# Making all low pieces of weights on VectorE in the second mixer and in the first mixer's output product

## The chip, the cores and the metric

The kernel runs on one core of a Trainium2 chip. The metric is the device time of one execution in microseconds. In three runs the kernel before took 2084.22, 2087.37 and 2090.94 us; the median is 2087.37 us. The core has TensorE (matrix products), VectorE, ScalarE, GpSimd and SyncE, which here issues most of the transfers. The profile calls them PE, DVE, ACT, POOL and SP; PEld is TensorE's loading of weights.

## The reference, cut to what matters

A two-layer network works on 256 tokens of 2048 channels, with 256 more as context. Each layer has a mixer and a gated ConvFFN; both are preceded by an RMS norm with shift and scale, and multiplied by a gate, all of which come from a conditioning vector. Layer 0 has the first mixer, a convolution beside a state-space model; layer 1 has the second, a gated MLP over chunks of tokens:

```
def chunk_mlp_mixer(hn, w_in, ln_g, ln_b, sgu_w, sgu_b, w_out):
    z = jax.nn.gelu(hn @ w_in)
    u, v = jnp.split(z, 2, axis=-1)
    v = layer_norm(v, ln_g, ln_b)
    ...
    s = jnp.einsum('hqk,bnkhc->bnqhc', sgu_w.astype(v.dtype), v)
    ...
    return (u * s.reshape(bn, length, SGU_W)) @ w_out

sh1, sc1, g1, sh2, sc2, g2 = jnp.split(silu_c @ ada_w[layer] + ada_b[layer], 6, axis=-1)
h_lat = h_lat + g1[:, None, :] * mix
```

All is in 32-bit floats. `hn @ w_in` of the second mixer is 256 x 2048 by 2048 x 4096, its output product 256 x 2048 by 2048 x 2048. `silu_c @ ada_w` is one vector by 2048 x 12288 in each layer.

## The kernel before, in words

Every large product is done as three products of the faster 32-bit kind: a weight `raw` is split into a high piece `hi` (a rounded copy, ScalarE, line 129) and a low piece `lo` = `raw` - `hi` (line 132). The activations were split in the same way into `xh` and `xl` (or `ah` and `al`). TensorE then adds `xh` x `hi`, `xh` x `lo` and `xl` x `hi` (lines 136 to 138). A weight tile of 128 x 2048 is fetched by one transfer (line 156, four buffers `raw`) and is split in two halves of 128 x 1024, here called splits; `hi` and `lo` have three buffers each. Each split feeds twelve products: two tiles of 128 tokens, two column halves, three products.

A counter decides which engine makes a `lo`: every `pool_every`-th split goes to GpSimd, the others to VectorE. The value is set stage by stage in `even` and `program`: for the first three quarters of the first mixer's output product it is `PE3`, 4; from the first ConvFFN to the end of the program it is `PE5`, 2, so that the engines take turns.

Beside the splits VectorE does the norms, the state-space scans of the first mixer (line 766), the residual adds (lines 407, 408), the layer norm of `v` in the second mixer, and for three of the twelve conditioning vectors a product done by hand: slabs `rawa` of 128 x 1024 from `ada_w` (two buffers, line 239) are multiplied by the conditioning vector and added to `adacc` (line 241). The other conditioning vectors are done on TensorE (line 199).

A scheduler sets the order of instructions on each engine when the program is built, from priorities and modelled times: fetch and split of weights are raised by `ahead`, 200 or 250 places. Each engine, and the queue of SyncE that issues transfers, then works in that fixed order: an instruction that waits holds up all behind it.

Of the kernel before, what the change touches and what calls it, by code (L numbers as in the profile page):

```python
# [31 lines left out]
NB = LD // 2  # L32
PE1 = 3
PE2 = 1000000000
PE3 = 4
PE0 = 4
PE4 = 1000000000
ADA_G = 0
PE5 = 2
# [19 lines left out]
class Builder:  # L59
# [844 lines left out]
    def even(self):  # L904
# [157 lines left out]
        row = self.gate_row(0, 2)  # L1062
        self.pool_every = PE3
        self.out_proj(WO, h, row, mh, ml, q4[:3], None, (ADA_EO, 0.0), rate=RS[8])
# [232 lines left out]
    def program(self, stop=99):  # L1297
        nc, A = self.nc, self.A
        h, ssq = self.even()
        if stop == 1:  # L1300
            return dict(xh=self.mh, xl=self.ml)
        q4 = [(q, 4 * q) for q in range(4)]
        self.yp = self.ctx.enter_context(self.tc.tile_pool(name="yp", bufs=1))
        if stop == 2:
            return dict(h=h)
        self.pool_every = PE5
        self.ahead = AHEAD2
        for l in range(2):
            if l == 1:
                self.xh, self.xl = self.xpair()  # L1310
                self.ada_pump(ADA_B[1])
                self.norm_mod(h, ssq, 1, 0, self.xh, self.xl)
                ah = self.yp.tile([128, KT, 256], F32R, name="ah", tag="ah")
                al = self.yp.tile([128, KT, 256], F32R, name="al", tag="al")
                self.odd(ah, al)
                ssq = self.new_ssq()
                row = self.gate_row(1, 2)
                self.out_proj(A["o_w_out"], h, row, ah, al, q4, ssq, ADA_O2)
                if stop == 4:
                    return dict(h=h)  # L1320
            self.xh, self.xl = self.xpair()
            self.ada_pump(ADA_B[2 * l])
            self.norm_mod(h, ssq, l, 1, self.xh, self.xl)
            ssq = self.new_ssq()
            self.ffn(l, h, ssq, *(ADA_F0 if l == 0 else ADA_F1))
            if stop == 3 + 2 * l:
                return dict(h=h)
        with self.tc.high_priority(HP2):
            r = self.ssq_rms(ssq, D, "rn")
            for t in range(2):  # L1330
                for g in (0, 2):
                    c = slice(512 * g, 512 * g + 1024)
                    x = h[:, t, 512 * g:512 * g + 512]
                    nc.vector.tensor_scalar(x, x, r[:, t:t + 1], None, op0=OP.mult)
                    x = h[:, t, 512 * g + 512:512 * g + 1024]
                    nc.scalar.activation(x, x, AF.Copy, scale=r[:, t:t + 1])
                    nc.sync.dma_start(self.out[t, :, c], h[:, t, c])
# [98 lines left out]
```

## Time and profile before

| | us |
|---|---|
| median of three runs | 2087.37 |
| the profiled execution | 2086.91 |
| its span | 2085.1 |
| TensorE busy, whole span | 1979.5 |
| second mixer, 1156 to 1512 us: TensorE busy | 322.71 of 356 |
| second mixer: VectorE busy | 238.91 of 356 |
| second mixer: GpSimd busy | 127.65 of 356 |
| first mixer's product and scans, 380 to 515 us: TensorE busy | 125.39 of 135 |

All durations come from the one profiled execution. The second mixer's stage is bounded here by the norm ahead of it and the norm of the ConvFFN behind it. Where an idle time is given in brackets, the profile names what ended it. Transfers are named after the tile that they fill.

### The profile page before, as it was taken

Reading aid. Unit: us, or ns where it says so; the run is one execution under the profiler, and the core shown is the slowest. Engines: PE = TensorE matmul, PEld = TensorE weight load, DVE = VectorE, ACT = ScalarE, POOL = GpSimd, SP = SyncE. Lnnn points to the kernel's source line nnn. Section 1 sums busy time; section 2 is a strip of 40 time slices with the busy share of each in tenths; the row PEclk is TensorE's granted clock in tenths of the full one; section 3 lists DMA queues with packets and bytes.
Section 4 is the critical chain, followed back from the end, with each engine's and each line's share of the span. In section 5 each row is a group of like instructions: output and inputs, shape, how many; then the busy total and the mean of one; then the engine's idle time right before and its main releaser. Section 6 shows DMA issues by size and latency. Waiting matters only on the chain.

```text
span 2085.1 us, 26177 instructions
## 1 busy us (share of the span) xinstructions
PE 1979.5 (95%) x9736; PEld 1479.9 (71%) x9736; DVE 1407.6 (68%) x2444; ACT 961.4 (46%) x1320; POOL 724.8 (35%) x376
## 2 busy tenths in 40 slices
PE   5999999899899999999999899989899999999997
PEld 2567676567577677777777677767577888888886
DVE  6467376666768996367865757566747885378874
ACT  3354353734445453355544543333355554455553
POOL 4311143011043443444344334434233344444443
PEclk8999999999999999999999999999999999999999
DMA  9993553876886888656577788787866655555552
GB/s 383 400 356 123 196 194 142 320 287 245 302 323 254 293 328 322 246 219 222 207 257 264 270 308 301 272 302 263 322 241 230 232 181 193 183 187 188 190 201 102
DMA packets 85530, 523.66 MB, mean 251 GB/s; under 512 B 10679, under 2 KB 11112, under 8 KB 29720
## 3 DMA queue, kind: packets, MB, share of 16 engines
q1 hardware_dynamic: 82198, 517.84, 67.1%
q10 hardware_dynamic: 2820, 2.99, 0.4%
q8 instruction: 76, 1.25, 0.2%
q0 software_dynamic: 384, 1.16, 0.1%
q14 instruction: 52, 0.42, 0.1%
HBM read 519.83 MB, written 2.13 MB: 250 GB/s over the span
## 4 chain that ended last, share of the span: by engine, by line
PE 76%; DVE 10%; DMA 5%; issue 5%; ACT 2%; POOL 2%; ACTq 0%; SPq 0%; POOLq 0%; DVEq 0%
PE mm L136 21%; PE mm L137 21%; PE mm L138 21%; PE ad L199 4%; DVE lo L132 2%; DVE adacc L241 2%; POOL lo L132 2%; DMA rawa<-in_ada_w 2%; PE tp L1209 1%; PE ad L472 1%; PE tp L877 1%; DVE w L766 1%; PE ms L794 1%; DMA glub<-in_glu_b 1%; PE tp L738 1%
## 5 line engine op out<-in xcount | busy, mean ns | idle before, releaser
L132 POOL TENSOR_TENSOR lo<-raw,hi 128x1024 fp32r<-128x1024 f32 x253 | 628.7, 2485 | 1224.5 <-ACT hi L129 1202.7
L129 ACT ACTIVATE hi<-raw 128x1024 fp32r<-128x1024 f32 x568 | 598.8, 1059 | 823.8 <-PE mm L138 638.9
L137 PE MATMUL mm<-lo,xh 128*128 128x512 f32 x1632 | 644.9, 395 | 21.5 <-DVE lo L132 21.5
L136 PE MATMUL mm<-hi,xh 128*128 128x512 f32 x1632 | 656.6, 404 | 1.6 <-ACT hi L129 1.6
L138 PE MATMUL mm<-hi,xl 128*128 128x512 f32 x1632 | 643.4, 394 | 1.6 <-DVE xl L399 1.6
L132 DVE TENSOR_TENSOR lo<-raw,hi 128x1024 fp32r<-128x1024 f32 x315 | 402.4, 1281 | 323.8 <-ACT hi L129 323.2
L136 PEld LDWEIGHTS mm<-hi,xh 128*128 128x128 f32 x1632 | 307.9, 190 | 126.3 <-issue 56.5
L137 PEld LDWEIGHTS mm<-lo,xh 128*128 128x128 f32 x1632 | 309.8, 190 | 89.0 <-DVE lo L132 29.4
L138 PEld LDWEIGHTS mm<-hi,xl 128*128 128x128 f32 x1632 | 309.4, 190 | 69.8 <-DVE xl L399 2.4
L136 PE MATMUL mm<-hi,ah 128*128 128x512 f32 x640 | 256.0, 401 | 2.9 <-ACT hi L129 2.8
L137 PE MATMUL mm<-lo,ah 128*128 128x512 f32 x640 | 255.8, 400 | 2.5 <-DVE lo L132 2.4
L138 PE MATMUL mm<-hi,al 128*128 128x512 f32 x640 | 254.7, 398 | 0.0
L241 DVE SCALAR_TENSOR_TENSOR adacc<-rawa,cst,adacc 128x1024 f32<-128x1024 f32 x96 | 163.0, 1708 | 54.9 <-DMA rawa<-in_ada_w 52.2
L1225 DVE SCALAR_TENSOR_TENSOR ca<-tp,fcw,ca 128x189 f32<-128x189 f32 (+2 forms) x512 | 179.0, 419 | 28.4 <-ACT ca L1212 28.4
L1225 DVE SCALAR_TENSOR_TENSOR cg<-tp,fcw,cg 128x189 f32<-128x189 f32 (+2 forms) x512 | 179.3, 419 | 21.8 <-ACT cg L1212 21.8
L136 PEld LDWEIGHTS mm<-hi,ah 128*128 128x128 f32 x640 | 120.5, 189 | 47.4 <-issue 14.2
L137 PEld LDWEIGHTS mm<-lo,ah 128*128 128x128 f32 x640 | 121.0, 189 | 33.7 <-DVE lo L132 5.1
L138 PEld LDWEIGHTS mm<-hi,al 128*128 128x128 f32 x640 | 121.1, 189 | 30.3 <-issue 1.7
L199 PE MATMUL ad<-raw,cst 128*32 128x512 f32 x896 | 125.0, 605 | 0.9 <-DMA raw<-in_ada_w 0.9
L407 DVE TENSOR_TENSOR wk<-mm,grow 128x512 f32<-128x512 f32 x56 | 38.2, 684 | 47.0 <-PE mm L138 47.0
L1277 DVE TENSOR_TENSOR al<-ca,ah 128x512 fp32r<-128x512 f32 x32 | 53.4, 1669 | 19.8 <-ACT ah L1276 19.7
L408 DVE TENSOR_TENSOR h<-h,wk 128x512 f32<-128x512 f32 x56 | 55.2, 989 | 1.3
(272 smaller groups left out, 1430.4 us busy)
## 6 DMA issues: line engine op xcount, KB each, us to landing
raw<-in_ada_w SPq DMA_DIRECT2D x132, 1024.0 KB, 5.8
raw<-in_f_w_in SPq DMA_DIRECT2D x128, 1024.0 KB, 4.9
raw<-in_f_w_out SPq DMA_DIRECT2D x64, 1024.0 KB, 5.0
rawa<-in_ada_w SPq DMA_DIRECT2D x96, 512.0 KB, 5.7
raw<-in_o_w_in SPq DMA_DIRECT2D x32, 1024.0 KB, 6.0
raw<-in_e_w_in SPq DMA_DIRECT2D x28, 1024.0 KB, 7.1
raw<-in_e_w_out SPq DMA_DIRECT2D x16, 1024.0 KB, 5.1
raw<-in_o_w_out SPq DMA_DIRECT2D x16, 1024.0 KB, 7.4
```

Of the source, the lines that this page charges most:

```text
L129: nc.scalar.activation(hi, raw, AF.Copy)
L132: eng.tensor_sub(lo, raw, hi.bitcast(F32))
L136: nc.tensor.matmul(ps, xh, wh, start=first, stop=False)
L137: nc.tensor.matmul(ps, xh, wl, start=False, stop=False)
L138: nc.tensor.matmul(ps, xl, wh, start=False, stop=last)
L199: nc.tensor.matmul(st["ps"][32 * j:32 * j + 32, :], self.cst[:, kt], raw[:, 512 * j:512 * j + 512], start=kt == 0, stop=kt == KT - 1, tile ...
L241: nc.vector.scalar_tensor_tensor(a, raw, self.cst[:, kt, 0:1], a, op0=OP.mult, op1=OP.add)
L407: nc.vector.tensor_mul(m, ps[t], row[:, c])
L408: nc.vector.tensor_add(h[:, t, c], h[:, t, c], m)
L472: nc.tensor.matmul(st["ps"][32 * j:32 * j + 32, :n], self.cst[:, no * s + o], raw[:, c:c + n], start=s == 0 and o < 2, stop=s == 16 // no ...
L1225: nc.vector.scalar_tensor_tensor(oo, s[:, y0 + dy:y1 + dy, x0 + dx:x1 + dx], w, oo, op0=OP.mult, op1=OP.add)
L1277: nc.vector.tensor_sub(al[:, kt:kt + 2], a, ah[:, kt:kt + 2].bitcast(F32))
```

## The change

```
-PE3 = 4
+PE3 = 1000000000
...
+                self.pool_every = 10 ** 9
                 self.odd(ah, al)
                 ssq = self.new_ssq()
                 row = self.gate_row(1, 2)
                 self.out_proj(A["o_w_out"], h, row, ah, al, q4, ssq, ADA_O2)
                 if stop == 4:
                     return dict(h=h)
+            self.pool_every = PE5
             self.xh, self.xl = self.xpair()
```

With a `pool_every` that the counter never reaches, all `lo` of the first mixer's output product and of the second mixer (input product, `odd`, and output product) are made on VectorE. The counter itself goes on, so that the ConvFFNs divide their splits as before. No instruction is added or removed; but the scheduler sets a new order.

On VectorE, in the first mixer's output product, where the residual of one group of columns (`wk`, `h`) meets the scans (line 766) of the state-space part:

```order
 L766 SCALAR_TENSOR_TENSOR w<-s5q,w 128x128
 L408 TENSOR_TENSOR h<-h,wk 128x512
-L766 SCALAR_TENSOR_TENSOR w<-s5q,w 128x128 x2
-L132 TENSOR_TENSOR lo<-raw,hi 128x1024
-L766 SCALAR_TENSOR_TENSOR w<-s5q,w 128x128 x2
+L132 TENSOR_TENSOR lo<-raw,hi 128x1024 x2
+L766 SCALAR_TENSOR_TENSOR w<-s5q,w 128x128 x6
```

Two low pieces stand where one stood, ahead of two scans that stood ahead of it.

On VectorE, in the second mixer, in the chain of small steps that makes the layer norm's factor `rnr`:

```order
 L319 SCALAR_TENSOR_TENSOR rnr<-rnt,rnj 128x2
 L317 TENSOR_TENSOR rnt<-rnr 128x2
+L132 TENSOR_TENSOR lo<-raw,hi 128x1024
 L318 SCALAR_TENSOR_TENSOR rnt<-rnt,ov 128x2
 L319 SCALAR_TENSOR_TENSOR rnr<-rnt,rnr 128x2
```

A low piece now stands in the middle of the chain.

On VectorE, towards the end of the second mixer's output product, before the change:

```order
L241 SCALAR_TENSOR_TENSOR adacc<-rawa,cst,adacc 128x1024 x2
L132 TENSOR_TENSOR lo<-raw,hi 128x1024
L241 SCALAR_TENSOR_TENSOR adacc<-rawa,cst,adacc 128x1024 x2
L132 TENSOR_TENSOR lo<-raw,hi 128x1024
L241 SCALAR_TENSOR_TENSOR adacc<-rawa,cst,adacc 128x1024
L132 TENSOR_TENSOR lo<-raw,hi 128x1024
```

and at the same place with the change:

```order
L241 SCALAR_TENSOR_TENSOR adacc<-rawa,cst,adacc 128x1024
L132 TENSOR_TENSOR lo<-raw,hi 128x1024
L241 SCALAR_TENSOR_TENSOR adacc<-rawa,cst,adacc 128x1024
L132 TENSOR_TENSOR lo<-raw,hi 128x1024
L241 SCALAR_TENSOR_TENSOR adacc<-rawa,cst,adacc 128x1024
L132 TENSOR_TENSOR lo<-raw,hi 128x1024 x2
L241 SCALAR_TENSOR_TENSOR adacc<-rawa,cst,adacc 128x1024
```

Pairs of `adacc` with one `lo` between them have become single `adacc` and single `lo` in turn.

## Rows read from the trace of the kernel before

**Rows 1.** The page, busy time: us, share of the span, count.

```profile
PE 1979.5 (95%) x9736; PEld 1479.9 (71%) x9736; DVE 1407.6 (68%) x2444; ACT 961.4 (46%) x1320; POOL 724.8 (35%) x376
```

**Rows 2.** Busy time by stretch: PE, PEld, DVE, ACT, POOL; clock; DMA share; GB/s.

```profile
1280.00:1290.00 10.00, 7.14 (x25) 5.41 (x24) 9.83 (x17) 1.94 (x3) 2.38 (x1) 0.83 0.62 235
1156.00:1512.00 356.00, 322.71 (x1444) 238.00 (x1442) 238.91 (x277) 139.16 (x176) 127.65 (x49) 0.97 0.80 291
380.00:515.00 135.00, 125.39 (x863) 90.73 (x861) 90.13 (x151) 65.94 (x105) 16.57 (x7) 0.99 0.74 276
```

**Rows 3.** Groups by line, 1156 to 1512 us: count, busy us, mean ns, idle before.

```profile
L132 POOL TENSOR_TENSOR lo<-raw,hi 128x1024 fp32r<-128x1024 f32 x48 | 125.8, 2622 | 214.0 <-ACT hi L129 211.5 <-issue 2.5
...
L241 DVE SCALAR_TENSOR_TENSOR adacc<-rawa,cst,adacc 128x1024 f32<-128x1024 f32 x59 | 101.7, 1734 | 39.0 <-DMA rawa<-in_ada_w 39.0
L129 ACT ACTIVATE hi<-raw 128x1024 fp32r<-128x1024 f32 x96 | 100.8, 1058 | 175.3 <-PE mm L138 135.4 <-DMA raw<-in_o_w_out 24.8 <-PE ad L199 7.1
L132 DVE TENSOR_TENSOR lo<-raw,hi 128x1024 fp32r<-128x1024 f32 x48 | 64.4, 1342 | 47.8 <-ACT hi L129 47.7
```

**Rows 4.** Timeline (start, us) of VectorE and GpSimd; line 132: min/median/max ns.

```profile
1189.36 1.27 DVE L241 SCALAR_TENSOR_TENSOR adacc<-rawa,cst,adacc 128x1024 f32<-128x1024 f32 x1
...
1191.22 3.42 DVE L241 SCALAR_TENSOR_TENSOR adacc<-rawa,cst,adacc 128x1024 f32<-128x1024 f32 x1
...
1189.55 4.01 POOL L132 TENSOR_TENSOR lo<-raw,hi 128x1024 fp32r<-128x1024 f32 x1 [5.75 <-ACT hi L129]
...
L132 DVE TENSOR_TENSOR lo<-raw,hi x48: 1209/1224/3409, 1163.7 to 1494.2; 128x1024 fp32r<-128x1024 f32 x48
```

**Rows 5.** TensorE's idle times in the second mixer, in brackets with their end.

```profile
1176.14 0.50 PE L138 MATMUL mm<-hi,xl 128*128 128x512 f32 x1 [1.56 <-DVE xl L399]
...
1185.65 0.66 PE L387 MATMUL tp<-ident,wk 128*128 128x128 f32 x4 [1.38 <-DVE modr L398]
...
1205.08 0.50 PE L137 MATMUL mm<-lo,xh 128*128 128x512 f32 x1 [2.88 <-DVE lo L132]
...
1236.07 0.50 PE L137 MATMUL mm<-lo,xh 128*128 128x512 f32 x1 [1.08 <-DVE lo L132]
...
1465.85 0.87 PE L136 MATMUL mm<-hi,ah 128*128 128x512 f32 x2 [2.77 <-ACT hi L129]
...
1492.99 1.05 PE L248 MATMUL ms<-adacc,ones 128*32 128x512 f32 x4 [1.69 <-DVE adacc L241]
```

**Rows 6.** TensorE's idle times in the first mixer; eight scans, undisturbed and lengthened.

```profile
424.77 0.50 PE L137 MATMUL mm<-lo,xh 128*128 128x512 f32 x1 [3.44 <-DVE lo L132]
...
465.76 0.51 PE L137 MATMUL mm<-lo,xh 128*128 128x512 f32 x1 [0.88 <-DVE lo L132]
...
490.13 0.50 PE L137 MATMUL mm<-lo,xh 128*128 128x512 f32 x1 [1.31 <-DVE lo L132]
...
398.20 2.62 DVE L766 TENSOR_TENSOR_SCAN w<-s5q,w 128x128 f32<-128x128 f32 x8
...
482.56 4.80 DVE L766 TENSOR_TENSOR_SCAN w<-s5q,w 128x128 f32<-128x128 f32 x8
```

**Rows 7.** VectorE's waits for slabs, 1156 to 1510: sum, times, longest; two of them.

```profile
DVE adacc L241 <- DMA rawa<-in_ada_w: 39.0, 17, 5.3
...
1201.07 2.83 DVE L241 SCALAR_TENSOR_TENSOR adacc<-rawa,cst,adacc 128x1024 f32<-128x1024 f32 x1 [5.29 <-DMA rawa<-in_ada_w]
...
1353.16 1.28 DVE L241 SCALAR_TENSOR_TENSOR adacc<-rawa,cst,adacc 128x1024 f32<-128x1024 f32 x1 [5.24 <-DMA rawa<-in_ada_w]
```

**Rows 8.** TensorE at full pace: two products, 30 apart.

```profile
1195.01 0.39 PE L136 MATMUL mm<-hi,xh 128*128 128x512 f32 x1
...
1201.81 0.39 PE L136 MATMUL mm<-hi,xh 128*128 128x512 f32 x1
```

**Rows 9.** The chain of waits from 1340 to 1400 us, shares by line.

```profile
by line: DMA rawa<-in_ada_w 35.2%; DVE adacc L241 18.2%; issue 10.5%; PE mm L136 6.4%; PE mm L137 6.3%; PE mm L138 6.1%; POOL lo L132 4.0%; PE tp L1187 3.1%; PE ms L1170 2.8%; ACT hi L129 1.8%; PE tp L1170 1.4%; PE tp L213 1.1%; DVE lo L132
```

**Rows 10.** The page, issues of slabs: count, KB, median us to landing.

```profile
rawa<-in_ada_w SPq DMA_DIRECT2D x96, 512.0 KB, 5.7
```

More of the change, by code (lines that the diff above doesn't have):

```diff
@@ L34 @@
 PE2 = 1000000000
-PE3 = 4
+PE3 = 1000000000
 PE0 = 4
@@ L1314, in program @@
                 al = self.yp.tile([128, KT, 256], F32R, name="al", tag="al")
+                self.pool_every = 10 ** 9
                 self.odd(ah, al)
@@ L1320, in program @@
                     return dict(h=h)
+            self.pool_every = PE5
             self.xh, self.xl = self.xpair()
```

## The prediction

> **What bounds the kernel now.** I read the page first. TensorE is busy 95% of the span and VectorE 68% [rows 1], so what a change on VectorE and GpSimd can be worth lies in the 5% where TensorE stands still. Next I cut the span into the two stretches that the change touches. In the second mixer, 1156 to 1512 us, TensorE is busy for 322.71 of 356 us, so 33 us are idle; GpSimd is busy 127.65 us there. In the first mixer's output product, 380 to 515 us, 9.6 us of 135 are idle [rows 2]. The groups by line then show who works there: of the 96 low pieces `lo` of the second mixer 48 are made on VectorE and 48 on GpSimd, and VectorE also does 59 `adacc` steps, each on a slab `rawa` that a transfer brings [rows 3].
>
> Then the timeline, where the reader is to compare the same instruction with and without a neighbour on GpSimd [rows 4]. An `adacc` takes 1.27 us when GpSimd is quiet and 3.42 us when it starts while a `lo` is in work there: it ends 1.08 us after that `lo` ends (1193.56). So VectorE does not run slower; it stands until GpSimd is done. An undisturbed `lo` takes 1.22 us. One such wait costs VectorE up to 3.42 - 1.27 = 2.15 us. In sum, over the stage, the 59 adacc carry 101.7 - 59 x 1.27 = 26.8 us of it and the 48 lo 64.4 - 48 x 1.22 = 5.8 us [rows 3, 4].
>
> Last, TensorE's idle times in the two stretches with what ended them; of ten that matter in the second mixer rows 5 show six. Most end with a `lo`, an `xl` or a `wk` of VectorE that stood behind an instruction lengthened in this way.
>
> **The change part by part.** Built, the new order has 369 `lo` on VectorE where 315 were, 54 more: 48 in the second mixer and 6 in the first mixer's product. ScalarE's `hi`, TensorE's products and all transfers stay the same in number.
>
> *VectorE's load.* Added in the second mixer: 48 x 1.22 = 58.6 us. Given back: 26.8 + 5.8 = 32.6 us from the two groups above alone. VectorE goes from 238.9 to about 264.9 us of 356, 74%. On average it hides beside TensorE's work, so the load as such costs nothing; the order in which it comes is another matter (below).
>
> *Second mixer, the waits that go.* From each of the ten idle times I take the smaller of the idle time and one lock wait of 2.15 us. Four are shorter than a lock wait: 1.56 and 1.38 (the norm ahead of the stage), 1.08 and 1.69. Six are longer, at 1205 (the first, 2.88), 1285 (behind the small layer-norm chain, in whose middle the new order sets a `lo`), 1315, 1359, 1399 and 1465 us (the last, 2.77) [rows 5]: 6 x 2.15 = 12.9. Together 18.6 us. At three of them, 1315, 1399 and 1465, a transfer was late as well, and is next; there I count half, which takes off 3.2. Left: 15.4 us.
>
> *First mixer.* Three idle times end with a `lo` [rows 6]. Ahead of the second and third stands a pair or a set of scans that waited for GpSimd (eight scans took 4.80 us, where eight others took 2.62 [rows 6]); with 2.18 us gone, 0.88 and 1.31 vanish. At 424.77 the new order keeps the `lo` behind the four residual steps, and only two scans move behind it, by the same row 2 x 2.62 / 8 = 0.7 us. Together 2.9 us. The six added pieces, 7.3 us, stand against the 2.18 us that each such scan no longer waits.
>
> *What it costs.* On GpSimd a `lo` could pass an `adacc` that waits for its slab. Now each stands behind one. VectorE waits 39.0 us for slabs, 17 times [rows 7]. A `lo` has room: with three buffers it may come two splits after its buffer came free, and a split of twelve products is 2.72 us (30 products from 1195.01 to 1201.81, 0.227 us each [rows 8]), so 5.44 less 1.06 for `hi` and 1.22 for itself, 3.16 us. The short waits fit in that. Five waits are over 4 us, 4.85 in the mean; the first and the last of them are shown [rows 7]. Each costs 4.85 - 3.16 = 1.7 us, if a moved `lo` is behind it: 8.5 us. From below this cost is 0 (where the scheduler set the `lo` ahead of the `adacc`, as it does in several places), from above the five waits whole, 24 us; I take the value between, since the new order has both patterns.
>
> *Clock.* After idle times of about 2.8 us the slice at 1280 to 1290 shows a granted clock of 0.83 with 25 products, where at 0.227 us there is room for 44 [rows 2, 8]; the clock thus takes up to 1.7 us more at each of four such places. I count nothing for it, since shorter idle times may still lower it, and leave up to 6.8 us in the range.
>
> *A rule that speaks against the change.* VectorE is busy for 9.83 of 10 us in the slice at 1280 us, and for 0.67 of the stage [rows 2]. The Trainium skill (Perfetto Trace Analysis, section Optimizing Scalar/DVE Operations) advises moving work from VectorE to ScalarE or even GpSimd once VectorE is saturated, and adds that between VectorE and GpSimd it might not help since they share a read port. By its first half the moved pieces would make VectorE the bound, which is the slower rival below; by its second half, and by rows 4, part of that saturation is waiting for GpSimd itself.
>
> *Sum.* 15.4 + 2.9 - 8.5 = 9.8 us less. Against the profiled execution's own 2086.91 us, which is 0.5 us below the median of the runs, that is 2077.
>
> **Rivals.** *The slabs take over (2083 us).* The chain of waits from 1340 to 1400 us is 35% `rawa` transfer and 18% adacc [rows 9]; a slab lands 5.7 us after its issue [rows 10]. If at every place where a transfer is near the path it becomes the last, only the places without one pay: 1.56 + 1.38 + 1.08 + 2.15 and the first mixer's 2.9, 9.1 us, less half the cost above, 4.2: about 4.9 less, near 2082 to 2083. For it: most of VectorE's own idle time with an adacc next is put down to a slab [rows 7]. Against: a lengthened adacc frees its buffer late, so some of that lateness is GpSimd's.
>
> *VectorE's order throttles TensorE (2095 us).* With two slab buffers, a slab is replaced at the soonest after its adacc (1.27 us) and the landing (5.7 us [rows 10]): 7.0 us for two, 3.5 a slab. In the new order 22 of the intervals between two adacc hold exactly one `lo`. Where these run in a row, TensorE gets a split every 3.5 us and not 2.72: 22 x 0.78 = 17.2 us. If the waits above give back only half, 9.2, the kernel is 8 us slower, 2095. It decides from the point where two slab buffers turn around slower than TensorE uses up two splits (5.44 us). For it: rows 7 and 9. Against: 59 slabs in 356 us are one per 6.0 us, so the queue of slabs is dense only in places; and before, each pair of adacc with a lock wait turned around slower still.
>
> *Nothing (2087 us).* Idle times only move. That the pieces would not move is ruled out by the new order. For this rival speaks only that 95% of TensorE's time is untouched.
>
> **How the numbers follow.** Chances: forecast 0.60, slabs 0.22, throttle 0.13, nothing 0.05. A difference of 0.3%, 6.3 us, is about what a measurement of this kernel can tell from no change; faster begins at 2081. The forecast's own range, with the cost from 0 to double and the clock, is 2065 to 2086; of its 0.60 some 0.52 lie below 2081, of the slabs' 0.22 some 0.08. Faster 0.60, same 0.26, slower 0.14. The range to quote takes in the slabs' case and "nothing", and leaves out most of the throttle: 2065 to 2090.
>
> **What would show it.** Right: no adacc or lo above 1.3 us from 1156 to 1512, GpSimd idle there but for one MEMSET, the eight scans back at 2.62 us, the idle times at the norm and at the layer-norm chain gone, the stage 8 to 10 us shorter, and the first mixer's product about 3. The slabs' rival: TensorE still waits about 25 us in the stage, behind `lo` that stood behind an adacc with its wait put down to `rawa`. The throttle: runs of split, adacc, split with TensorE idle 0.8 us in each. What would make me wrong outright is TensorE waiting longer for `lo` than before although no VectorE instruction is lengthened.

## The result, and the profile after

The changed kernel takes 2060.11 us (median of four runs, 2058.89 to 2063.06) where before takes 2085.8 us (four runs, 2082.74 to 2090.94). The ratio is 0.9876, with an interval from 0.9859 to 0.9894: 25.7 us less. The forecast was 2077, with a range from 2065 to 2090: the measured time lies below it. The direction was right, and the gain was 2.6 times the 9.8 us of the sum. The profiled execution took 2059.81 us, 27.1 less than that of before.

The page after: busy time by engine (us, share of the span, count).

```profile
PE 1970.3 (96%) x9736; PEld 1469.7 (71%) x9736; DVE 1418.0 (69%) x2498; ACT 961.4 (47%) x1320; POOL 585.5 (28%) x322
```

VectorE does 54 instructions more and is busy only 10.4 us longer [rows 1], though 54 pieces of 1.22 us are 65.9 us of work. The other 55 us are, by this subtraction, time in which it stood behind GpSimd, written down as busy. The second mixer's stretch of [rows 2], moved along with the work, and the two slices inside it below full clock (columns as there; a third, at 0.56 from 1480 to 1490 us, lies for the most part in the norm behind the stage):

```profile
1148.00:1484.00 336.00, 315.69 (x1438) 234.75 (x1440) 246.99 (x323) 138.72 (x175) 1.81 (x1) 0.98 0.85 308
1150.00:1160.00 10.00, 5.22 (x31) 2.85 (x24) 9.43 (x30) 6.00 (x10) 0.00 (x0) 0.84 0.99 392
1310.00:1320.00 10.00, 7.79 (x22) 3.81 (x23) 5.14 (x5) 2.63 (x4) 1.79 (x1) 0.66 0.67 256
```

In the second mixer GpSimd is left with one MEMSET of 1.81 us. VectorE's load is 247 us in 336, 73%; 264.9 us, or 74% of a stage 20 us longer, were forecast. The 48 added pieces are 58.6 us of work and raise it by 8.1, so 50.5 us came back, where the prediction counted 32.6 from `adacc` and `lo` alone. The groups by line of that stretch after (count, busy us, mean ns, idle before), which answer [rows 3]:

```profile
L132 DVE TENSOR_TENSOR lo<-raw,hi 128x1024 fp32r<-128x1024 f32 x96 | 116.8, 1221 | 40.6 <-ACT hi L129 40.4
...
L241 DVE SCALAR_TENSOR_TENSOR adacc<-rawa,cst,adacc 128x1024 f32<-128x1024 f32 x59 | 75.1, 1278 | 27.3 <-DMA rawa<-in_ada_w 27.2
```

Both means stand at the undisturbed times, 1.22 and 1.28 us. And the slabs, whose transfers the change leaves as they are, are waited for 27.2 us instead of 39.0 [rows 7]; the longest of these waits went from 5.3 to 3.5:

```profile
DVE adacc L241 <- DMA rawa<-in_ada_w: 27.2, 21, 3.5
```

TensorE's waits of the second mixer, after and then before (sum in us, times, longest):

```profile
PE tp L387 <- DVE rnr L344: 5.7, 2, 3.5
PE ms L248 <- DVE adacc L241: 4.0, 1, 4.0
PE mm L137 <- DVE lo L132: 3.7, 7, 1.0
PE mm L136 <- ACT hi L129: 2.6, 3, 1.6
PE tp L1187 <- DVE wk L1177: 2.2, 2, 1.9
PE tp L387 <- ACT wk L371: 2.0, 2, 1.3
```

Before, 1156 to 1512 us:

```profile
PE mm L137 <- DVE lo L132: 12.0, 9, 2.9
PE tp L387 <- DVE rnr L344: 4.8, 2, 3.4
PE tp L1187 <- DVE wk L1177: 4.3, 2, 3.1
PE tp L213 <- DVE wk L207: 3.1, 1, 3.1
PE mm L136 <- ACT hi L129: 2.8, 1, 2.8
PE ms L248 <- DVE adacc L241: 1.7, 1, 1.7
PE mm L138 <- DVE xl L399: 1.6, 1, 1.6
PE tp L387 <- DVE modr L398: 1.4, 1, 1.4
PE tp L387 <- ACT wk L371: 1.2, 2, 0.9
```

The sum falls from 32.9 to 20.2 us. Of what is left, 7.7 us (`rnr` and `wk` of line 371) stand at the two norms that bound the stage, at one place each, and 4.0 are one new wait. The timeline after shows it, first TensorE's, then the two `adacc` and the last `lo` ahead of it on VectorE (start, us, idle before in brackets):

```profile
1312.21 1.92 PE L248 MATMUL ms<-adacc,ones 128*32 128x512 f32 x4 [4.04 <-DVE adacc L241]
...
1305.93 1.27 DVE L241 SCALAR_TENSOR_TENSOR adacc<-rawa,cst,adacc 128x1024 f32<-128x1024 f32 x1
1307.13 1.21 DVE L132 TENSOR_TENSOR lo<-raw,hi 128x1024 fp32r<-128x1024 f32 x1
1310.88 1.28 DVE L241 SCALAR_TENSOR_TENSOR adacc<-rawa,cst,adacc 128x1024 f32<-128x1024 f32 x1 [2.53 <-DMA rawa<-in_ada_w]
```

The last `adacc` of a vector waits 2.53 us for its slab, and the closing sum of that vector waits for it.

*Where the 27 us went.* Compare the start of the same product in both traces. At 403 us, just ahead of the first place where VectorE's order differs, after is already 6.5 us early. This is no effect of the change: e1 (below), whose first mixer is as before, is 6.2 early there, and e4, whose order up to there is that of after, 1.2. Part of it is a slow slice of before, whose granted clock was 0.66 from 280 to 290 us; in after it was 1.00 from 250 to 330. The first mixer then gives 4.4 us at two places (2.8 and 1.6), and the norm at 555 us takes 2.5 back. Through the first ConvFFN the lead stays at 8.4 us. The second mixer gives 18.7 us: 27.1 at its end, which the last ConvFFN keeps. So 20.6 of the 27.1 us of this pair of traces stand where the change is.

### The profile page after: what moved, and what is told of

Same layout as the page of the kernel before. It is cut to its first block, busy times and chain, and to the rows that moved or that the text cites. A ratio compares the mean times of both kernels' runs of the same rounds, so it can differ in the third digit from the quotient of the medians.

```text
span 2058.0 us, 26106 instructions
## 1 busy us (share of the span) xinstructions
PE 1970.3 (96%) x9736; PEld 1469.7 (71%) x9736; DVE 1418.0 (69%) x2498; ACT 961.4 (47%) x1320; POOL 585.5 (28%) x322
## 4 chain that ended last, share of the span: by engine, by line
PE 83%; DVE 8%; DMA 5%; ACT 2%; issue 1%; ACTq 0%; SPq 0%; DVEq 0%
PE mm L136 24%; PE mm L137 23%; PE mm L138 23%; PE ad L199 4%; DVE lo L132 2%; DMA rawa<-in_ada_w 2%; DVE adacc L241 1%; PE tp L1209 1%; PE tp L877 1%; PE ad L472 1%; PE tp L387 1%; DMA glub<-in_glu_b 1%; DMA lnrow<-in_o_ln 1%; PE tp L738 1%; PE ms L794 1%
## 5 line engine op out<-in xcount | busy, mean ns | idle before, releaser
L132 POOL TENSOR_TENSOR lo<-raw,hi 128x1024 fp32r<-128x1024 f32 x199 | 488.8, 2456 | 1024.6 <-ACT hi L129 1014.0
L132 DVE TENSOR_TENSOR lo<-raw,hi 128x1024 fp32r<-128x1024 f32 x369 | 462.3, 1258 | 318.3 <-ACT hi L129 317.8
L241 DVE SCALAR_TENSOR_TENSOR adacc<-rawa,cst,adacc 128x1024 f32<-128x1024 f32 x96 | 136.6, 1429 | 43.6 <-DMA rawa<-in_ada_w 41.0
L137 PEld LDWEIGHTS mm<-lo,ah 128*128 128x128 f32 x640 | 120.6, 188 | 32.6 <-DVE lo L132 4.0
L229 POOL MEMSET adacc<- 128x2048 f32 x3 | 5.4, 1810 | 332.5 <-PE ms L248 175.1
```

The source lines that it names most:

```text
L132: eng.tensor_sub(lo, raw, hi.bitcast(F32))
L137: nc.tensor.matmul(ps, xh, wl, start=False, stop=False)
L241: nc.vector.scalar_tensor_tensor(a, raw, self.cst[:, kt, 0:1], a, op0=OP.mult, op1=OP.add)
```

## Experiments

Theory: a GpSimd `lo` holds up the VectorE instructions that start beside it, and these hold up TensorE; the gain is the holding that is gone. Rivals: the gain comes from the new order of VectorE's instructions (or from GpSimd's late pieces), and the slabs rather than the hold set the time.

### Which part carries it: e1_second_only, e2_first_only, e8_odd_only

```
e1, from after:   -PE3 = 1000000000   +PE3 = 4
e2, from before:  -PE3 = 4            +PE3 = 1000000000
e8, from after, behind self.odd(ah, al):
                  +self.pool_every = PE5
```

> Only the second mixer's part of the change: in the first mixer's output product every fourth low piece is on GpSimd again. In the two traces the product starts came 18.7 us closer between 1156 and 1512 us and some 3 us in the first mixer; another 5 us of the difference lie ahead of the first changed instruction. Theory that the second mixer carries the change: 2085.8 - 19 = 2067, between 2064 and 2070, and the time from the second mixer's first product to the ConvFFN's as in the changed kernel. Rival that the first mixer's part carries more than it shows in one trace (the 5 us ahead of it included): 2070 to 2074.

> Only the first mixer's part: the second mixer shares the low pieces between the engines as before. Theory from the two traces: 3 us faster than before, 2080 to 2084 against a kernel before of 2085.8; idle of TensorE at the three places of the first mixer (3.44, 0.88, 1.31 us) down to 0.5 or gone. Rival that the 5 us ahead of the change belong to it: 2077 to 2079.

> The changed kernel, but the second mixer's output product shares its low pieces with GpSimd again (every second one); the input product keeps all on VectorE. In the two traces the input product's stretch carried about 15 of the second mixer's 19 us, the output product's 4. Theory that the price is per GpSimd piece and per place: 2063 to 2067. Rival that the output product, whose VectorE work is densest in slabs, carries half: 2067 to 2072; that it carries nothing: 2060.

e1 took 2064.17 us, ratio 0.9889 (0.986 to 0.9917); e2 2084.88, ratio 0.9997 (0.9974 to 1.002); e8 2066.73, ratio 0.9921 (0.9894 to 0.9948). So the second mixer alone carries most of the 25.7 us, as e1's theory had it: 20.9 by the medians, 17 to 29 by the ratio's interval. What the first mixer brings is inside e2's interval: e2 missed its 2080 to 2084, and its time decides nothing. Its trace does show the two steps, -2.8 and -1.6 us at the same products as in after, and in e1, where the first mixer is as before, they are absent (-0.1 and 0.0). In e8 the output product of the second mixer has its GpSimd pieces back: the stage then gains 11.0 us by products instead of 18.7, so by these two traces 7.7 of it come from the output product. The 2066.73 us lie where its theory and its rival meet, and don't tell them apart.

### The hold itself: e3_sub_beside, e9_half_beside, e4_memset_beside

Each keeps the new order on all engines but GpSimd (in their traces VectorE does the same 2498 instructions in the same order as in after), and gives GpSimd something to do beside the stage, once `hi` is there: in e3 a subtraction as large as a `lo` with every second split, in e9 with every fourth, in e4 four MEMSETs that take 2.1 us and read nothing large. A copy of one column of `hi` ahead of them lets them start only when `hi` is there. The edit, shortened:

```
 def split, from after (side is set in the second mixer only):
+if self.side and self.split_n % 2 == 0:          # e9: % 4
+    j = yp.tile([128, 1024], bf16, ...)          # e4: [128, 512], F32
+    nc.gpsimd.tensor_copy(j[:, :1], hi[:, :1])
+    nc.gpsimd.tensor_sub(j, xh[:, :4], xl[:, :4])
+                                  # e4 instead: 4 x nc.gpsimd.memset(j, 0.0)
```

> The changed kernel, with the order on VectorE, ScalarE, TensorE and of the transfers untouched, but beside every second split of the second mixer GpSimd does a subtraction of two 128 x 1024 operands into a tile that nothing reads. No low piece depends on GpSimd. Theory that VectorE stands while a GpSimd subtraction reads its operands: VectorE's adacc and lo are lengthened again by up to 2.15 us, and half or more of the second mixer's 18.7 us is lost again: 2070 to 2080. Rival that GpSimd's pieces were late (2.4 us against 1.2 us) and freed the weight buffers late: no change, 2059 to 2062, with lengthened VectorE instructions at most beside the path. Rival that the new order on VectorE made the gain: also 2059 to 2062.

> As the kernel with the subtraction beside, but GpSimd fills a tile four times (128 x 512 each, some 2.1 us together) instead of subtracting: GpSimd is as busy, but reads nothing larger than one column. Theory that it is the reading of GpSimd's operands that holds VectorE: 2059 to 2063, no adacc above 1.4 us. Rival that any work of GpSimd holds VectorE, or that its instructions cost through semaphores: as slow as the subtraction, 2070 to 2080.

> As the kernel with a subtraction beside every second split of the second mixer, but beside every fourth only: 24 subtractions, not 48; the order on all other engines is that of the changed kernel. The 48 cost 41 us by the medians (2101.19 against 2060.11). Theory that each subtraction costs the same, 0.86 us, wherever it stands: 2060 + 20 = 2080, between 2077 and 2084. Rival that a few waits are absorbed by the buffers and only dense ones reach TensorE: 2064 to 2074.

e3 took 2101.19 us, ratio 1.0063 (1.0037 to 1.009): slower than before, and 21 us above what its theory gave. e9 took 2072.96, ratio 0.9932 (0.9915 to 0.995): the theory of a constant price missed, and its rival's 2064 to 2074 held. e4 took 2059.2, ratio 0.9861 (0.9826 to 0.9895): as after, and as its theory had it. The groups of e3 in the second mixer, and its longest sum of TensorE waits:

```profile
L133 DVE TENSOR_TENSOR lo<-raw,hi 128x1024 fp32r<-128x1024 f32 x96 | 146.5, 1537 | 23.5 <-ACT hi L130 23.5
L138 POOL TENSOR_TENSOR side<-xh,xl 128x1024 bf16<-128x1024 f32 x48 | 138.1, 2878 | 11.5 <-DVE xl L405 7.7
L247 DVE SCALAR_TENSOR_TENSOR adacc<-rawa,cst,adacc 128x1024 f32<-128x1024 f32 x59 | 104.0, 1770 | 14.6 <-DMA rawa<-in_ada_w 14.6
...
PE mm L143 <- DVE lo L133: 24.8, 23, 2.9
```

The same groups of e4:

```profile
L133 DVE TENSOR_TENSOR lo<-raw,hi 128x1024 fp32r<-128x1024 f32 x97 | 118.3, 1222 | 43.4 <-ACT hi L130 43.0
...
L130 ACT ACTIVATE hi<-raw 128x1024 fp32r<-128x1024 f32 x98 | 103.2, 1060 | 162.0 <-PE mm L144 102.0 <-DMA raw<-in_o_w_out 32.2 <-POOL side L138 19.3
L138 POOL MEMSET side<- 128x512 f32 x192 | 102.2, 532 | 11.1
L247 DVE SCALAR_TENSOR_TENSOR adacc<-rawa,cst,adacc 128x1024 f32<-128x1024 f32 x60 | 76.4, 1279 | 24.9 <-DMA rawa<-in_ada_w 24.9
```

And of e9:

```profile
L133 DVE TENSOR_TENSOR lo<-raw,hi 128x1024 fp32r<-128x1024 f32 x97 | 134.6, 1392 | 36.4 <-ACT hi L130 36.4
L247 DVE SCALAR_TENSOR_TENSOR adacc<-rawa,cst,adacc 128x1024 f32<-128x1024 f32 x59 | 89.2, 1518 | 13.6 <-DMA rawa<-in_ada_w 13.6
L138 POOL TENSOR_TENSOR side<-xh,xl 128x1024 bf16<-128x1024 f32 x24 | 69.0, 2876 | 1.9
```

The reader is to look at the means of `adacc` and `lo`. Under 138 us of subtractions they rise to 1770 and 1537 ns, under 102 us of MEMSETs they stay at 1279 and 1222. The order on VectorE is the same in both, and no result of GpSimd is waited for by TensorE in either. So the new order and late GpSimd pieces fall as causes. The copy of one column, which stands in all three, falls too: in e4 ScalarE waits 19.3 us for GpSimd to let go of `hi`, and it costs nothing. What is left is the subtraction, which reads two large operands where the MEMSET reads none; that it is the reading, and not another trait of the subtraction, no run here takes apart. The Trainium skill (SBUF — State Buffer, section SBUF: two separate sides) says that GpSimd and VectorE share a pair of ports as an exclusive lock for a whole instruction, and that a VectorE instruction with two operands in SBUF takes part only against a GpSimd one that reads SBUF. e3 and e4 agree with it, on both halves.

The price is not a constant for each piece. By the ratios 48 subtractions cost 0.0187 x 2086 = 39 us (0.8 each), 24 cost 0.0056 x 2086 = 12 us (0.5 each), with 5 to 7 us of uncertainty on either. VectorE itself is held in proportion: by the means above, beyond 1278 and 1221 ns, 59 us in e3 and 31 in e9. So it is on the way to TensorE that the price bends; that the buffers take up the first holds is argued, not shown. And e3 is slower than before, since it has all 96 `lo` on VectorE and the hold too: moving the pieces is worth its price only because the hold goes with them.

### The slabs: e5_three_slabs, e6_before_three_slabs, e7_fin_later

```
e5 from after, e6 from before:
-raw = self.yp.tile([128, 1024], F32, name="rawa", tag="rawa", bufs=2)
+raw = self.yp.tile([128, 1024], F32, name="rawa", tag="rawa", bufs=3)
-pw = self.s5pw = self.cp.tile(...)
+pw = self.s5pw = self.s5c_.tile(...)          # makes the room
e7 from after:
-... + [(0.5, lambda: None), (0.0, fin)]
+... + [(2.0, lambda: None), (0.0, fin)]
```

> The changed kernel with three slab buffers in place of two (a small table of the first mixer is moved to another pool to make room; nothing is left out). It takes away VectorE's waiting for slabs, 27.2 us in the second mixer of the changed kernel. Theory that slabs now cost TensorE about 4 us of idle time and 3 us of clock at one place (the last two slabs of a conditioning vector, 4.04 us): 2053 to 2058. Rival that what is left of the slab waits lies beside the path: 2059 to 2062. The rival of the prediction, that slabs throttle the stage now: below 2050.

> The kernel before with three slab buffers and the low pieces shared with GpSimd as before. Theory that GpSimd's subtractions, by making VectorE stand, cause the second mixer's losses: adacc stays at 1.7 us in the mean, and of the 19 us that the change gave there 6 or less come: 2079 to 2086. Rival that late slabs caused them and the change helped by freeing slabs earlier: 10 us or more come: 2068 to 2076.

> The changed kernel, but the step that closes a conditioning vector's product (the four products from adacc, at which TensorE waits 4.04 us in the second mixer) is queued three splits later; everything is computed. Theory that this one wait and the half clock behind it are the whole price of putting all low pieces on VectorE: the 4.04 us go, and 3 us of clock: 2052 to 2057. Rival that the wait turns up at the next product that needs VectorE: 2058 to 2062.

e6 took 2082.55 us, ratio 0.9983 (0.9964 to 1.0003). If slabs had set the time of before, a third buffer should have brought what the change brought; it brought nothing that can be told, as its theory had it. But the group of e6 shows that VectorE still waits 33.6 us for slabs (39.0 before), so this run alone does not rule the slabs out. e3 and e9 speak against them: there the waits for slabs are down to 14.6 and 13.6 us, and the kernel is slower than after. And in e6 the hold is still there:

```profile
L241 DVE SCALAR_TENSOR_TENSOR adacc<-rawa,cst,adacc 128x1024 f32<-128x1024 f32 x59 | 97.9, 1672 | 33.7 <-DMA rawa<-in_ada_w 33.6
```

e5 took 2055.49 us, ratio 0.9868 (0.9848 to 0.9887), an interval that overlaps that of after. In its trace the second mixer gains 32.2 us by products (after: 18.7), and some 6 are lost at norms and in the first ConvFFN. Its waits for slabs, from 1160 to 1480 us:

```profile
DVE adacc L241 <- DMA rawa<-in_ada_w: 11.3, 8, 2.9
```

e7 was to give the last slab of a vector more room. Both expectations missed: it took 2075.16 us, ratio 0.9961 (0.9944 to 0.9977), some 15 worse than after. The 4.04 us wait at 1312 is gone; by products some 8 us are lost against after around 1440 us, and some 6 in the norm behind the stage. That the slabs, pushed into other places, are the cause is argued; VectorE waits 34.5 us for them. TensorE's waits at the close of a vector in the second mixer of e7:

```profile
PE ms L248 <- DVE adacc L241: 3.7, 2, 2.0
```

So that wait can't be costed by itself as long as the plan of the slabs is shifted to remove it.

### How far it goes: e10_first_stages, e11_everywhere, e12_three_slabs_first

```
e10 from after, e12 from e5:
-PE1 = 3     +PE1 = 1000000000
-PE0 = 4     +PE0 = 1000000000
e11 from after:
-PE5 = 2     +PE5 = 1000000000
```

> The changed kernel, and all low pieces of the first mixer's input product on VectorE too (12 or so that GpSimd made there). TensorE waits 2.6 us for low pieces between 60 and 380 us. Theory that the price is per GpSimd piece beside a busy VectorE: 2 us faster, 2057 to 2060. Rival that VectorE is too full of norms and products there: 2061 to 2066.

> The changed kernel, and all low pieces of the two ConvFFNs on VectorE as well. In the kernel before, TensorE was busy for 547.58 of 550 us and 530.00 of 530 there, so there is nothing to win but a few us; VectorE, busy for 0.72 of it with GpSimd's share taken off, gets some 180 pieces of 1.22 us more. Theory that what GpSimd makes VectorE wait offsets most of what is added: 2058 to 2066. Rival that the depthwise convolutions and the pieces fill VectorE and TensorE waits: 2075 or more.

> Three slab buffers (2055.49 alone) and all low pieces of the first mixer's input product on VectorE too: if the two gains add, 2053 to 2055; if the first stages lose, 2056 to 2062.

e10 took 2056.17 us, ratio 0.9859 (0.983 to 0.9887), just below both its ranges; that it beats after is not shown, since the intervals overlap. e11 took 2063.27, ratio 0.9894 (0.9865 to 0.9922), inside its theory's range, and not to be told from after by its time. Its trace, by products, shows two halves of opposite sign against after, some -3.5 us in the first ConvFFN and some +12 in the second. In the second TensorE waits for `ah`, which it never does in after, and VectorE is busy 448.78 us of 550 where it was 385.97 (waits of e11 from 1480 to 2062 us):

```profile
PE mm L136 <- ACT ah L1276: 7.1, 2, 5.4
```

The window of e11, with the columns of rows 2:

```profile
1480.00:2030.00 550.00, 542.84 (x2426) 435.74 (x2427) 448.78 (x784) 275.35 (x346) 0.00 (x0) 0.99 0.55 196
```

So there, by this pair of traces, GpSimd's pieces are worth more than the hold costs. That VectorE's load is the reason for the late `ah` is argued from its 82%; no run takes it apart.

e12 joins e5 and e10: 2050.6 us, ratio 0.9828 (0.98 to 0.9856). Its interval lies below that of after, so it beats both kernels, by more than either of its ranges gave. Its median is the lowest; that it beats e5 or e10 is not shown, since the intervals overlap.

## Why the prediction was right in kind and short in size

*Right.* The mechanism of rows 4 was the cause, as e3 against e4 shows. VectorE's load came out at 73%. That its share of the stage comes so near the 74% is in part luck: the load fell 18 us short of the forecast, and the stage got 20 us shorter with it. The signs that "what would show it" named for the forecast came: no lengthened `adacc` or `lo`, GpSimd idle but for one MEMSET, the eight scans back at 2.63 us, and the idle times of 1.56 and 1.38 at the norm, and those at 1205 and 1285, gone. The two sizes named with them did not: the stage is 18.7 us shorter and not 8 to 10, the first mixer's product 4.4 and not about 3. The throttle did not come: TensorE waits 3.7 us for `lo` in seven pieces, the longest 1.0, against 12.0 before.

*The step that failed is the sum: the mechanism was right, and four of its terms were mis-sized, all to the same side.*

1. "Left: 15.4 us" of waits that go. Apart from the waits for `rnr` and `wk` at the norms and from the new wait, TensorE's waits fall from 26.9 to 8.5, by 18.4 us. Four of the idle times before, and the two of them that are left after (not adjacent in the traces):

```profile
1285.20 0.66 PE L137 MATMUL mm<-lo,xh 128*128 128x512 f32 x1 [2.85 <-DVE lo L132]
1315.40 0.50 PE L137 MATMUL mm<-lo,xh 128*128 128x512 f32 x1 [2.70 <-DVE lo L132]
1359.55 0.66 PE L213 MATMUL tp<-ident,wk 128*128 128x128 f32 x4 [3.12 <-DVE wk L207]
1399.54 0.66 PE L1187 MATMUL tp<-ident,wk 128*128 128x128 f32 x4 [3.10 <-DVE wk L1177]
...
1375.44 0.55 PE L1187 MATMUL tp<-ident,wk 128*128 128x128 f32 x3 [1.89 <-DVE wk L1177]
1441.08 0.73 PE L136 MATMUL mm<-hi,ah 128*128 128x512 f32 x2 [1.63 <-ACT hi L129]
```

At 1205, 1285 and 1359 the idle times of 2.88, 2.85 and 3.12 us are gone whole, where the sum allowed one lock wait of 2.15 for each: 2.4 us. Ahead of the one at 1285 two held instructions stood in a row in before, an `adacc` of 2.82 us and a step of the `rnr` chain that else takes 0.16:

```profile
1275.45 2.82 DVE L241 SCALAR_TENSOR_TENSOR adacc<-rawa,cst,adacc 128x1024 f32<-128x1024 f32 x1
1280.65 2.32 DVE L319 SCALAR_TENSOR_TENSOR rnr<-rnt,rnr 128x2 f32<-128x2 f32 x1
```

"There I count half, which takes off 3.2" was wrong at one of its three places: 2.70 us at 1315 are gone whole, 1.6 more than counted. At 1399 and 1465 the idle times fell from 3.10 to 1.89 and from 2.77 to 1.63, which is about the half. Whether the transfers there were late because a held `adacc` frees its slab's buffer late stays open: the waits for slabs fell by 11.8 us with the hold gone, but in e3, where the hold is back, they are shorter still (14.6 us). Small waits at other places take some 1 us of these gains back.

2. "8.5 us" for `lo` behind `adacc` that wait for slabs. The longest such wait is now 3.5 us, hardly above the room of 3.16 that the prediction gave a `lo`, so almost none of it gets through. In its place stand the 4.04 us at the close of a vector, a place that the prediction did not name, and 1.7 us more at the norms: 5.7 us.

3. "I count nothing for it" (the clock). Before, the slices below full clock lose up to (0.34 + 4 x 0.17) x 10 = 10.2 us of the stage, those at 1280 us [rows 2] and these:

```profile
1160.00:1170.00 10.00, 5.62 (x20) 3.63 (x17) 9.87 (x29) 7.55 (x12) 2.45 (x1) 0.66 0.98 401
1310.00:1320.00 10.00, 7.30 (x25) 5.54 (x25) 10.00 (x11) 2.09 (x3) 3.33 (x1) 0.83 0.96 372
1360.00:1370.00 10.00, 10.00 (x43) 8.31 (x42) 5.53 (x10) 2.74 (x4) 1.53 (x1) 0.83 0.48 188
1460.00:1470.00 10.00, 6.85 (x23) 4.78 (x22) 6.40 (x4) 2.00 (x2) 2.46 (x1) 0.83 0.88 325
```

After, the two slices inside the stage lose up to (0.16 + 0.34) x 10 = 5.0. Full clock is 2.4 GHz, and the mean of such a slice lies between it and 1.2. By these upper figures the clock gave 5.2 us back. TensorE's busy time bears the size out: 322.71 us in the stage before and 315.69 after, with 6 instructions of some 0.23 us fewer in the stretch, so 5.6 us less for the same work.

4. The first mixer's 2.9 us came out at 4.4. The idle time of 3.44 at 424.77, for which only 0.7 us was counted, went to 0.47: the pair of scans ahead of it had taken 2.94 us, and the undisturbed pairs beside it 0.73, so VectorE was late by one hold there too, as at the other two places. With that idle time went the slow slice behind it: the granted clock is 0.83 from 420 to 430 us before, and 1.00 from 410 to 420 after.

By these terms the second mixer is 18.4 - 5.7 + 5.2 = 17.9 us of the 18.7 that the products show, and with the first mixer's 4.4 the sum is 22.3. The runs say 25.7. What is left, some 3 us, or 5 with the 2.5 that the norm at 555 us takes back, is of the size of the differences between traces of one order (by products the second mixer gains 18.7 us in after and 22 in e4), and stays open.

*The range.* The text says that it goes by the cost from 0 to double and the clock. With the cost at 0 and the 6.8 us of clock that is 2086.9 - 15.4 - 2.9 - 6.8 = 2061.8, not 2065, and even so the measured 2060.1 lies below it: the waits that go were bounded too low as well.

*The rule weighed.* The Trainium skill (Perfetto Trace Analysis, section Optimizing Scalar/DVE Operations) would have work moved off a saturated VectorE, and says that GpSimd might not help. Here the saturation was in good part the hold: with GpSimd's pieces taken back VectorE is at 73% and the kernel 25.7 us faster, so the second half decides for this stage. e11's second ConvFFN shows the other side.

## What to carry to other kernels

Price a GpSimd instruction that reads SBUF by what it makes VectorE wait, not by its own end. Where an idle time of TensorE is longer than one hold, look whether several held instructions stand ahead of it before capping the gain at one; and where the idle time goes, count the slice's clock with it. Here the move paid in the second mixer, and in the second ConvFFN, by one trace, it did not, so it is tried stage by stage.

## What the runs showed of the hardware that was not expected

- The hold leaves no trace beside GpSimd's MEMSET (532 ns for 128x512): `adacc` 1279 ns beside 192 of them, 1278 beside none; beside 48 subtractions, 1770.
- The hold's price rises faster than its count: 24 subtractions cost 12 us, 48 cost 39, though VectorE is held about half as long beside the 24.
- A third slab buffer alone was worth nothing measurable in before (0.9983), though 39.0 us of waits stood against the slabs [rows 7]; 33.6 of them were left. The change by itself took them down to 27.2.
